# The head of a streaming-encoder layer: where the modulation sums, the rotary tables and the LayerNorm scales are made

## The chip, the cores and the metric

One core of one Trainium2 chip runs the whole layer: batch 1, 512 positions, model width 1024, all in float32. The metric is the device time of one execution in microseconds (us); lower is better. The kernel before takes 1024.28 us (median of three runs, 1021.66 to 1024.99).

## What is computed

The layer has a token mixer and a gated MLP with a convolution. Both are modulated by a condition c, and both end in a residual LayerNorm. The change touches only what comes ahead of the token mixer's large matmuls: the modulation by c, the LayerNorm of x, the tables for the rotary embedding, and the first 704 columns of the input projection.

```python
def _rope_tables(pos):
    freqs = ROPE_THETA ** (-jnp.arange(0, QK_ROPE, 2, dtype=jnp.float32) / QK_ROPE)
    ang = pos.astype(jnp.float32)[..., None] * freqs
    return jnp.cos(ang), jnp.sin(ang)

def _modulate(x, shift, scale):
    return _layer_norm(x) * (1.0 + scale[:, None, :]) + shift[:, None, :]

def reference(x, c, pos, ...):
    cos, sin = _rope_tables(pos)
    c_act = jax.nn.silu(c)
    mod = c_act @ w_ada[l] + b_ada[l]
    sh_t, sc_t, gt_t, sh_f, sc_f, gt_f = jnp.split(mod, 6, axis=-1)
    h = _modulate(x, sh_t, sc_t)
    y = _token_mixer(h, cos, sin, w_in[l], ...)
    ...
```

Positions start at a random number up to 8191, so the angles have to be brought into one period before the sine is taken.

## The kernel before

A matmul in the kernel's precision is three passes: each operand is split into a high part (rounded to the fast float32 format) and a low part (what the rounding lost), and high times low, low times high and high times high are added in one PSUM bank. ScalarE (ACT) writes the high part, and VectorE (DVE) or GpSimd (POOL) subtracts to get the low part.

The head works in eight pieces, j = 0 to 7, one for each block of 128 channels of the model width. `first_loads(j)` (L177) issues on SyncE's queue (SP) four 256 KB tiles of the modulation weights (`ada`), which hold shift and scale columns of this block for all 1024 rows of c, and two tiles of input-projection weights (`w0`: 448 columns of latents, 256 columns of a gate). Tiles come from one pool of 48 buffers, so a load may have to wait until an older tile has been read for the last time.

`first_modulation(j)` (L186) makes the sum over c's rows on DVE: the weights lie with 128 rows on the partitions, and for each of the eight groups of rows one instruction multiplies a 128x256 half tile by a column of silu(c) and adds it to one of two running sums (two plain multiplications, L199, and six multiply-adds, L201). A last addition (L205) joins the two sums in `acc[0]`. The sum over the 128 partitions is still open then.

`prepare(j)` (L309) splits the `w0` weights (L318 on ACT, L319 on POOL), closes the sum over the partitions with two one-column matmuls against a column of ones (`pm`, L325; each call shows as two instructions in the trace), adds the bias on ACT (`md`, L330), transposes the normalised x of this block with four matmuls (`pt`, L336), and writes the modulated, transposed block twice on ACT (high part L342, full value L343) and its low part on POOL (L344). The split of piece j+1 is ordered behind the last split of piece j with `issue_after`, which adds an order on one engine and no wait between engines.

`first_columns(j)` (L349) adds the block to four banks of latents (`lat`, eight matmuls on the high part L355 and L356, four on the low part L357), and `first_gates(j)` (L359) to two banks of a gate (`g0ps`, six matmuls, L97 to L99). All eight pieces add into the same banks, so these are complete only after piece 7. Then the kernel goes on with gate columns (`pg`), the latents' norms, rotary queries and attention.

Ahead of the pieces, x is loaded in eight tiles, DVE takes its statistics (L134, L122), and for each of the four row blocks POOL makes reciprocal root and offset in three tiny instructions (L113, L116, L125). ACT normalises the first half of x's columns (L219), POOL the second (`late_norm`, L229). Two `warm` matmuls (L225) follow the normalised tiles. The rotary tables (L379 to L413) are made on DVE behind the fifth modulation sum: 14 instructions reduce the angles (L393 to L398), two sines run on ACT (L404, L411), and two scaled copies on DVE (L412, L413).

The order of the instructions on each engine is a planner's: it runs its own model of time over the whole program and takes what is ready there by its place in the program, with the `issue_after` marks as fixed order. On the chip each engine then runs its list in that order, and an instruction that waits holds up all behind it.

Of the kernel before, what the change touches and what calls it, by code (L numbers as in the profile page):

```python
# [10 lines left out]
I32 = mybir.dt.int32  # L11
# [39 lines left out]
def trunk(ctx: ExitStack, tc: tile.TileContext, A, out):  # L51
# [95 lines left out]

# [7 lines left out]
    cols = const.tile([P, N_COLS], F32, name="cols")  # L155
    nc.scalar.dma_start(out=cols, in_=A["cols"])

# [13 lines left out]
    nc.vector.tensor_scalar_add(out=bmod[:, :, 1], in0=cols[:, C_SCT : C_SCT + 8], scalar1=1.0)  # L171

    first_raw = {}
    first_acc = {}
    add_done = []

# [9 lines left out]
    def first_modulation(j):  # L186
        adas, first_raw[j] = loads.pop(j)
        acct = act_t(f"acc{j}", F32)
        acc = [acct[:, :256], acct[:, 256:]]
        with ExitStack() as order:  # L190
            if add_done:
                order.enter_context(tc.issue_after(add_done[-1]))
            for q in range(4):
                ada = adas[q]
                for i in range(2):
                    k = 2 * q + i
                    src = ada[:, i * 256 : (i + 1) * 256]
                    if q == 0:
                        nc.vector.tensor_scalar_mul(out=acc[i], in0=src, scalar1=cact[:, k : k + 1])  # L199
                    else:  # L200
                        nc.vector.scalar_tensor_tensor(  # L201
                            out=acc[i], in0=src, scalar=cact[:, k : k + 1], in1=acc[i],
                            op0=ALU.mult, op1=ALU.add,
                        )
# [5 lines left out]
    kst = const.tile([P, N_CONST], F32, name="kst")  # L210
    nc.sync.dma_start(out=kst, in_=A["consts"])
    posi = const.tile([P, TT], I32, name="posi")
    nc.sync.dma_start(out=posi, in_=A["pos"])
    first_modulation(0)

# [1 line left out]
    xrs = [ln_stats(xs[t]) for t in range(TT)]  # L217
    for t in range(TT):
        nc.scalar.activation(  # L219
            xs[t][0], xs[t][0], AF.Identity, bias=xrs[t][:, 1:2], scale=xrs[t][:, 0:1]  # L220
        )

    warm = ps("warm")
    for t in (1, 2):
        nc.tensor.matmul(warm, ident, xs[t][0], start=True, stop=True)  # L225

    def late_norm():
        for t in range(TT):
# [6 lines left out]
    plan = []  # L235
# [32 lines left out]

# [1 line left out]
    def gate(b, m, pg=None):  # L270
# [28 lines left out]

# [1 line left out]
    lat = [ps(f"lat{t}") for t in range(TT)]  # L301
# [4 lines left out]
    split_done = []  # L306
    md_done = []

    def prepare(j):  # L309
        raws = first_raw[j]  # L310
        acc = first_acc[j]
        wh = wp.tile([P, D], F32R, name="w0h", tag="whi")
        wl = wp.tile([P, D], F32R, name="w0l", tag="wlo")
        with ExitStack() as order:
            for ins in split_done:
                order.enter_context(tc.issue_after(ins))
            for raw, a, b in ((raws[0], 0, NL), (raws[1], NL, NS)):
                nc.scalar.copy(out=wh[:, a:b], in_=raw[:, : b - a])  # L318
                nc.gpsimd.tensor_tensor(  # L319
                    out=wl[:, a:b], in0=raw[:, : b - a], in1=f(wh[:, a:b]), op=ALU.subtract  # L320
                )
        w0s.append((wh, wl))
        pm = ps("pm")
        for i in range(2):
            nc.tensor.matmul(  # L325
                pm[:, i : i + 1], acc[:, i * P : (i + 1) * P], ones[:, 0:1], start=True, stop=True
            )
# [5 lines left out]
        md_done.append(add_done[j])  # L333
# [12 lines left out]
        hT_hi.append(hh)  # L346
        hT_lo.append(hl)
# [29 lines left out]

# [1 line left out]
    with tc.issue_after(md_done[4]):  # L379
        posf = const.tile([P, TT], F32, name="posf")  # L380
        nc.vector.tensor_copy(out=posf, in_=posi)
        ang = const.tile([P, TT, 32], F32, name="ang")
        cosT = const.tile([P, TT, 32], F32, name="cosT")
        cosQ = const.tile([P, TT, 32], F32, name="cosQ")
        sinQ = const.tile([P, TT, 32], F32, name="sinQ")
        sinT = const.tile([P, TT, 32], F32, name="sinT")
        for t in range(TT):
            nc.vector.tensor_scalar_mul(
                out=ang[:, t, :], in0=kst[:, K_FREQ : K_FREQ + 32], scalar1=posf[:, t : t + 1]
            )  # L390
        kq = const.tile([P, TT, 32], F32, name="kq")
        for step in (COARSE, 1.0):
            nc.vector.tensor_scalar(  # L393
                out=kq, in0=ang, scalar1=INV_2PI, scalar2=MAGIC * step, op0=ALU.mult, op1=ALU.add
            )
            nc.vector.tensor_scalar_add(out=kq, in0=kq, scalar1=-MAGIC * step)
            for c2 in TWO_PI:
                nc.vector.scalar_tensor_tensor(  # L398
                    out=ang, in0=kq, scalar=-c2, in1=ang, op0=ALU.mult, op1=ALU.add
                )  # L400
        nc.vector.tensor_scalar(
            out=ang, in0=ang, scalar1=3.1415925, scalar2=-3.1415925, op0=ALU.min, op1=ALU.max
        )
        nc.scalar.activation(sinT, ang, AF.Sin)  # L404
        nc.vector.scalar_tensor_tensor(
            out=kq, in0=ang, scalar=-1.0, in1=ang, op0=ALU.mult, op1=ALU.max
        )
        nc.vector.tensor_scalar(
            out=kq, in0=kq, scalar1=-1.0, scalar2=1.5707963267948966, op0=ALU.mult, op1=ALU.add
        )  # L410
        nc.scalar.activation(cosT, kq, AF.Sin)  # L411
        nc.vector.tensor_scalar_mul(out=cosQ, in0=cosT, scalar1=SCALE)  # L412
        nc.vector.tensor_scalar_mul(out=sinQ, in0=sinT, scalar1=SCALE)  # L413


    th0 = [gate(0, m, g0psum[m]) for m in range(2)]
# [1 line left out]
    ss = const.tile([P, TT, 2], F32, name="ss")  # L418
# [55 lines left out]

# [1 line left out]
    qrs = []  # L476
# [51 lines left out]

# [1 line left out]
    V = {}  # L530
# [134 lines left out]

# [1 line left out]
    ada_state = {}  # L667
# [46 lines left out]

# [1 line left out]
    po_hi = [None] * KT  # L716
# [69 lines left out]

# [1 line left out]
    def uv_half(i, nm, hook=None):  # L788
# [56 lines left out]

# [1 line left out]
    sg_hi = []  # L847
# [79 lines left out]

# [1 line left out]
    lntg = row_tiles(2, act_t, "lntg")  # L929
# [211 lines left out]

# [1 line left out]
    pzs = {}  # L1143
# [203 lines left out]
```

## Time and profile before

| | |
|---|---|
| median of three runs | 1024.28 us |
| span of the profiled execution, first to last instruction | 1018.8 us |
| median less span (start and end outside the records) | 5.5 us |
| TensorE (PE) busy | 973.7 us, 96% of the span |
| VectorE (DVE) busy | 611.4 us, 60% |
| ScalarE (ACT) busy | 384.2 us, 38% |
| GpSimd (POOL) busy | 325.7 us, 32% |
| mean granted TensorE clock | 0.991 |

The profiled execution has no time of its own beside its span, so the span is set against the median of the runs. PE is busy nearly all the time, but its busy time is an upper figure, since matmuls overlap and their ends are modelled. What matters is the stretches in which it stands still, and these are listed by what ended them. DVE is the busiest engine of the first 62 us.

### The profile page before, as it was taken

The page shows a single profiled execution, that of the slowest core. Times are in us where ns is not written, and L with a number is a line of the kernel's source. Part 1 is how long each engine was busy: PE and PEld are TensorE (multiplying, and loading weights), DVE is VectorE, ACT ScalarE, POOL GpSimd, SP SyncE. Part 2 cuts the span into 40 slices and gives each one's busy share as a digit, 9 for nine tenths or more (in the row PEclk, how much of TensorE's full clock was granted, in tenths as well). Part 3 has the DMA queues.
Part 4 walks back from the last instruction along what each step waited for, and adds up shares of the span by engine and source line. Part 5 has one row for each costly group of instructions (what it writes and reads, how often), then busy time and mean ns, then how long its engine had stood idle before and what let it go on. Part 6 is the DMA issues. An engine that isn't in the chain of part 4 may idle for free.

```text
span 1018.8 us, 12189 instructions
## 1 busy us (share of the span) xinstructions
PE 973.7 (96%) x4496; PEld 797.4 (78%) x4496; DVE 611.4 (60%) x931; ACT 384.2 (38%) x650; POOL 325.7 (32%) x340
## 2 busy tenths in 40 slices
PE   4789999999999999999999999899999999999996
PEld 3677778777888877788888877898888888888885
DVE  7957555548446377763343578676666665633267
ACT  3365454542224322332322233664443443412221
POOL 5564111121242054120001575512111121466664
PEclk9999999999999999999999999999999999999998
DMA  9612111118324226652223255113433343342322
GB/s 336 259 40 91 47 50 50 57 42 279 114 83 124 89 80 211 202 184 87 79 83 104 83 169 203 42 62 113 136 124 112 116 145 85 99 137 94 103 83 83
DMA packets 45276, 119.20 MB, mean 117 GB/s; under 512 B 5280, under 2 KB 8736, under 8 KB 45216
## 3 DMA queue, kind: packets, MB, share of 16 engines
q1 hardware_dynamic: 45072, 118.30, 35.8%
q8 instruction: 35, 0.57, 0.2%
q14 instruction: 25, 0.20, 0.1%
q10 hardware_dynamic: 144, 0.12, 0.0%
HBM read 116.30 MB, written 2.10 MB: 116 GB/s over the span
## 4 chain that ended last, share of the span: by engine, by line
PE 73%; DVE 9%; POOL 6%; DMA 6%; issue 4%; ACT 2%; SPq 0%; DVEq 0%; POOLq 0%; ACTq 0%
PE pzu L97 7%; PE pzu L99 7%; PE pzu L98 7%; PE pg L98 4%; PE pyd L97 4%; PE pg L99 4%; PE pg L97 4%; PE pyd L99 4%; PE pyd L98 4%; PE pu L97 3%; PE pu L99 3%; PE pu L98 3%; PE py L98 2%; PE py L99 2%; PE py L97 2%
## 5 line engine op out<-in xcount | busy, mean ns | idle before, releaser
L1203 POOL TENSOR_TENSOR zc<-zc 128x512 f32<-128x512 f32 x22 | 32.8, 1489 | 178.9 <-ACT zc L1202 178.9
L936 POOL TENSOR_TENSOR d<-d,gtfb 128x512 f32<-128x512 f32 x44 | 72.8, 1677 | 41.9 <-DMA d<-in_wdn 39.5
L298 POOL TENSOR_TENSOR mg<-mg,th 128x512 f32<-128x512 f32 x16 | 25.0, 1562 | 139.7 <-DVE th L295 120.2
L1188 DVE SCALAR_TENSOR_TENSOR zc<-pzu,cols,zc 128x511 f32<-128x511 f32 x44 | 32.8, 747 | 52.4 <-ACT zc L1185 52.4
L1185 ACT ACTIVATE zc<-pzu,cols 128x512 f32<-128x512 f32 x44 | 34.2, 779 | 72.2 <-PE pzu L99 72.2
L941 DVE TENSOR_TENSOR dl<-d,dh 128x1024 fp32r<-128x1024 f32 x18 | 29.9, 1660 | 52.3 <-ACT dh L940 52.3
L679 DVE SCALAR_TENSOR_TENSOR ada<-adar,cact,ada 128x512 f32<-128x512 f32 x56 | 52.9, 970 | 13.2 <-DMA adar<-in_ada 13.2
L90 ACT CAST wbh<-wb 128x1024 fp32r<-128x1024 f32 x24 | 25.2, 1050 | 65.7 <-PE py L99 57.2
L91 DVE TENSOR_TENSOR wgl<-wg,wgh 128x1024 fp32r<-128x1024 f32 x22 | 27.3, 1243 | 35.3 <-ACT wgh L90 34.1
L91 DVE TENSOR_TENSOR wupl<-wup,wuph 128x1024 fp32r<-128x1024 f32 x38 | 46.6, 1227 | 0.0
L91 DVE TENSOR_TENSOR wbl<-wb,wbh 128x1024 fp32r<-128x1024 f32 x24 | 35.1, 1461 | 16.3 <-ACT wbh L90 16.1
L91 DVE TENSOR_TENSOR wsgl<-wsg,wsgh 128x1024 fp32r<-128x1024 f32 x16 | 19.6, 1223 | 39.4 <-ACT wsgh L90 39.4
L940 ACT CAST dh<-d 128x1024 fp32r<-128x1024 f32 x18 | 18.9, 1051 | 60.7 <-PE pyd L99 60.6
L90 ACT CAST wuph<-wup 128x1024 fp32r<-128x1024 f32 x38 | 39.5, 1039 | 0.0
L278 ACT ACTIVATE th<-pg 128x512 f32<-128x512 f32 x22 | 13.1, 597 | 61.8 <-PE pg L99 61.8
L113 POOL TENSOR_SCALAR pw<-mv 128x1 f32<-128x1 f32 x20 | 8.2, 408 | 82.5 <-DVE mv L122 69.6
L90 ACT CAST wsgh<-wsg 128x1024 fp32r<-128x1024 f32 x16 | 16.8, 1049 | 47.0 <-PE pu L99 44.9
L1192 DVE SCALAR_TENSOR_TENSOR zc<-pzu,cols,zc 128x510 f32<-128x510 f32 x44 | 32.7, 747 | 1.3
L936 POOL TENSOR_TENSOR o<-o,gttb 128x512 f32<-128x512 f32 x16 | 27.0, 1712 | 17.5 <-DVE th L295 9.8
L734 POOL TENSOR_TENSOR asum<-apad 128x527 f32<-128x527 f32 x8 | 9.1, 1141 | 59.2 <-ACT apad L729 25.9
L600 POOL TENSOR_SCALAR pe<-pe,mx 128x128 f32<-128x128 f32 (+3 forms) x32 | 17.4, 553 | 33.4 <-DVE mx L599 33.2
L201 DVE SCALAR_TENSOR_TENSOR acc<-ada,cact,acc 128x256 f32<-128x256 f32 x48 | 27.8, 638 | 0.0
(1369 smaller groups left out, 3230.0 us busy)
## 6 DMA issues: line engine op xcount, KB each, us to landing
wup<-in_wup SPq DMA_DIRECT2D x44, 512.0 KB, 3.5
adar<-in_ada SPq DMA_DIRECT2D x64, 256.0 KB, 3.8
wb<-in_wb SPq DMA_DIRECT2D x24, 512.0 KB, 3.5
wg<-in_wg SPq DMA_DIRECT2D x22, 512.0 KB, 3.5
d<-in_wdn SPq DMA_DIRECT2D x22, 512.0 KB, 3.5
ada<-in_ada SPq DMA_DIRECT2D x32, 256.0 KB, 4.8
wsg<-in_wsg SPq DMA_DIRECT2D x16, 512.0 KB, 3.5
wa<-in_wa SPq DMA_DIRECT2D x8, 512.0 KB, 3.5
```

The lines of the kernel that those rows point to most:

```text
L90: nc.scalar.copy(out=hi[:, :n], in_=raw[:, :n])
L91: nc.vector.tensor_tensor(out=lo[:, :n], in0=raw[:, :n], in1=f(hi[:, :n]), op=ALU.subtract)
L97: nc.tensor.matmul(o, wh, xl, start=start, stop=False)
L98: nc.tensor.matmul(o, wl, xh, start=False, stop=False)
L99: nc.tensor.matmul(o, wh, xh, start=False, stop=stop)
L679: nc.vector.scalar_tensor_tensor(out=acc[n], in0=src, scalar=cact[:, k : k + 1], in1=acc[n], op0=ALU.mult, op1=ALU.add,)
L936: nc.gpsimd.tensor_tensor(out=raw[:, c], in0=raw[:, c], in1=gt[n], op=ALU.mult)
L941: nc.vector.tensor_tensor(out=lo, in0=raw, in1=f(hi), op=ALU.subtract)
L1185: nc.scalar.activation(t, pz, AF.Identity, bias=cols[:, cc + 3 : cc + 4], scale=cols[:, cc + 2 : cc + 3])
L1188: nc.vector.scalar_tensor_tensor(out=t[:, 1:512], in0=pz[:, 0:511], scalar=cols[:, cc + 1 : cc + 2], in1=t[:, 1:512], op0=ALU.mult, op1=AL ...
L1192: nc.vector.scalar_tensor_tensor(out=t[:, 2:512], in0=pz[:, 0:510], scalar=cols[:, cc : cc + 1], in1=t[:, 2:512], op0=ALU.mult, op1=ALU.add,)
L1203: nc.gpsimd.tensor_tensor(out=val, in0=val, in1=gate, op=ALU.mult)
```

## The change

Six things change, all before the first gate columns:

1. The constants, the positions and the bias columns are loaded first, on ACT's queue. Before, constants and positions went on SP's queue behind the loads of piece 1.
2. The angles (position times frequency) are made on DVE ahead of x's statistics, their reduction right behind the statistics. The last three DVE steps and the two sines come in the loop's first turn, and the two scaled copies move from DVE to ACT.
3. For pieces 0 and 1 (`DIRECT = 2`) there is no DVE sum. `prepare` takes the raw weight tiles as stationary operands and a column of silu(c) as the moving one: eight matmul calls for shift and eight for scale, added in PSUM.
4. For pieces 2 to 7 the last addition (L205) goes. Both running sums are given to PE, which closes each of shift and scale with two calls in place of one.
5. The modulation of piece j+2 is entered in turn j, beside its loads, where before that of piece j+1 was.
6. LayerNorm's scales of x are made for two row blocks at a time: two POOL instructions and one DVE instruction where there were six on POOL. The second half of x is normalised on ACT, in the loop's second turn, where POOL did it before the loop.

```diff
+    kst = const.tile([P, N_CONST], F32, name="kst")
+    nc.scalar.dma_start(out=kst, in_=A["consts"])
+    posi = const.tile([P, TT], I32, name="posi")
+    nc.scalar.dma_start(out=posi, in_=A["pos"])
+    cols = const.tile([P, N_COLS], F32, name="cols")
+    nc.scalar.dma_start(out=cols, in_=A["cols"])
...
+    def sines():
+        nc.vector.tensor_scalar(
+            out=ang, in0=ang, scalar1=3.1415925, scalar2=-3.1415925, op0=ALU.min, op1=ALU.max
+        )
+        nc.scalar.activation(sinT, ang, AF.Sin)
...
+        nc.scalar.activation(cosT, kq, AF.Sin)
+        nc.scalar.activation(cosQ, cosT, AF.Copy, scale=SCALE)
+        nc.scalar.activation(sinQ, sinT, AF.Copy, scale=SCALE)
+
+    angles()
...
     def first_modulation(j):
         adas, first_raw[j] = loads.pop(j)
+        if j < DIRECT:
+            first_acc[j] = [
+                (adas[q][:, i * 256 : (i + 1) * 256], cact[:, 2 * q + i : 2 * q + i + 1])
+                for q in range(4) for i in range(2)
+            ]
+            return
...
-            add = nc.vector.tensor_tensor(out=acc[0], in0=acc[0], in1=acc[1], op=ALU.add)
-        add_done.append(add.ins)
-        first_acc[j] = acc[0]
+        last_acc[:] = [ins.ins]
+        first_acc[j] = [(a, ones[:, 0:1]) for a in acc]
...
+    def x_scales(a, b):
+        power(rsx[:, a:b, 0], mvx[:, a:b, 1], 1.0, LN_EPS, b - a)
+        nc.vector.scalar_tensor_tensor(
+            out=rsx[:, a:b, 1], in0=mvx[:, a:b, 0], scalar=-1.0, in1=rsx[:, a:b, 0],
+            op0=ALU.mult, op1=ALU.mult,
+        )
...
+    for t in range(TT):
+        stats = x_stats(t)
+        if t % 2:
+            x_scales(t - 1, t + 1)
+            for u in (t - 1, t):
+                x_norm(u, 0)
     first_modulation(0)
...
+    first_modulation(1)
+    with tc.issue_after(stats.ins):
+        for step in (COARSE, 1.0):
+            reduce_angles(step)
...
     def late_norm():
-        for t in range(TT):
-            nc.gpsimd.tensor_scalar(
-                out=xs[t][1], in0=xs[t][1], scalar1=xrs[t][:, 0:1], scalar2=xrs[t][:, 1:2],
-                op0=ALU.mult, op1=ALU.add,
-            )
+        with after_split():
+            for t in range(TT):
+                x_norm(t, 1)
...
         pm = ps("pm")
         for i in range(2):
-            nc.tensor.matmul(
-                pm[:, i : i + 1], acc[:, i * P : (i + 1) * P], ones[:, 0:1], start=True, stop=True
-            )
+            for part, (a, col) in enumerate(acc):
+                nc.tensor.matmul(
+                    pm[:, i : i + 1], a[:, i * P : (i + 1) * P], col,
+                    start=part == 0, stop=part == len(acc) - 1,
+                )
...
     prepare(0)
-    late_norm()
     for j in range(KT):
         if j + 2 < KT:
             loads[j + 2] = first_loads(j + 2)
-        if j + 1 < KT:
-            first_modulation(j + 1)
+            first_modulation(j + 2)
+        if j == 0:
+            with after_split():
+                sines()
+        if j == 1:
+            late_norm()
         first_columns(j)
```

## Rows read from the trace of the kernel before

**Rows 1.** Busy time of each engine by stretches of the whole span (stretch in us: its length, then busy us and instructions of each engine, granted TensorE clock, share of the DMA engines, GB/s).
```profile
0.00:69.50 69.50, 47.36 (x213) 38.64 (x214) 57.67 (x111) 29.59 (x70) 38.38 (x53) 0.98 0.61 219
69.50:200.00 130.50, 129.67 (x636) 103.01 (x635) 75.17 (x177) 68.72 (x161) 32.84 (x78) 1.00 0.19 62
```

**Rows 2.** The chain of waits that ended last, from 11 to 70 us, in order of time (start us, length us, what).
```profile
61.93 0.44 DVE acc L205
...
62.41 0.61 PE pm L325 x4
```

**Rows 3.** What PE waited for between 30 and 66 us (us in total, times, longest).
```profile
PE pm L325 <- DVE acc L205: 8.1, 4, 2.6
PE lat L355 <- ACT hT5h L342: 0.4, 1, 0.4
```

**Rows 4.** The timeline, PE's matmuls alone (start us, length us, line, operation; the step from one start to the next is what a matmul costs in a row).
```profile
19.43 0.71 PE L355 MATMUL lat<-w0l,hT0h 128*128 128x448 f32 x1 [1.02 <-POOL w0l L319]
...
22.55 0.85 PE L325 MATMUL pm<-ones,acc 128*128 128x1 f32 x4
23.26 0.92 PE L336 MATMUL pt<-ident,x 128*128 128x128 f32 x4
...
26.21 0.50 PE L325 MATMUL pm<-ones,acc 128*128 128x1 f32 x4
26.57 0.45 PE L355 MATMUL lat<-w0l,hT1h 128*128 128x448 f32 x1
...
28.65 1.06 PE L357 MATMUL lat<-w0h,hT1l 128*128 128x448 f32 x4
...
34.16 0.72 PE L355 MATMUL lat<-w0l,hT2h 128*128 128x448 f32 x1
...
37.76 1.06 PE L357 MATMUL lat<-w0h,hT2l 128*128 128x448 f32 x4
...
40.04 0.50 PE L325 MATMUL pm<-ones,acc 128*128 128x1 f32 x4
...
44.75 0.36 PE L355 MATMUL lat<-w0l,hT4h 128*128 128x448 f32 x1
...
65.53 0.36 PE L355 MATMUL lat<-w0l,hT7h 128*128 128x448 f32 x1
...
69.33 0.39 PE L97 MATMUL pg<-hT0l,wgh 128*128 128x512 f32 x1
```

**Rows 5.** Stretches of 1 us, columns as in rows 1; then PE's weight loads by line (operation, count, busy us, mean ns of one).
```profile
21.00:22.00 1.00, 1.00 (x4) 0.87 (x4) 1.00 (x2) 0.00 (x0) 1.00 (x2) 1.00 0.98 369
35.00:36.00 1.00, 1.00 (x4) 0.87 (x4) 1.00 (x3) 0.00 (x0) 0.00 (x0) 0.50 1.05 408
...
L356 PEld LDWEIGHTS lat<-w0h,hT0h 128*128 128x128 f32 x4 | 1.3, 331 | 0.1
...
L356 PEld LDWEIGHTS lat<-w0h,hT1h 128*128 128x128 f32 x4 | 0.8, 189 | 0.1
```

**Rows 6.** The one-column matmuls by the tile they write: duration ns min/median/max, first and last start.
```profile
L325 PEld LDWEIGHTS pm<-ones,acc x32: 185/192/334, 15.8 to 62.7; 128*128 128x128 f32 x32
L325 PE MATMUL pm<-ones,acc x32: 164/250/352, 16.6 to 62.8; 128*128 128x1 f32 x32
```

**Rows 7.** Groups of DVE, POOL and ACT instructions from 0 to 66 us (busy us, mean ns of one, idle before).
```profile
L201 DVE SCALAR_TENSOR_TENSOR acc<-ada,cact,acc 128x256 f32<-128x256 f32 x48 | 27.8, 638 | 0.0
L199 DVE TENSOR_SCALAR acc<-ada,cact 128x256 f32<-128x256 f32 x16 | 11.5, 757 | 0.0
L398 DVE SCALAR_TENSOR_TENSOR ang<-kq,ang 128x128 f32<-128x128 f32 x10 | 5.7, 573 | 0.2
...
L319 POOL TENSOR_TENSOR w0l<-w,w0h 128x448 fp32r<-128x448 f32 x8 | 10.2, 1273 | 0.2 <-ACT w0h L318 0.2
L319 POOL TENSOR_TENSOR w0l<-w,w0h 128x256 fp32r<-128x256 f32 x8 | 6.6, 824 | 0.0
L344 POOL TENSOR_TENSOR hT1l<-hfull,hT1h 128x512 fp32r<-128x512 f32 x1 | 1.3, 1287 | 2.6 <-ACT hfull L343 2.6
...
L318 ACT CAST w0h<-w 128x448 fp32r<-128x448 f32 x8 | 4.5, 563 | 3.6 <-issue 3.6
L330 ACT ACTIVATE md<-pm,bmod 128x1 f32<-128x1 f32 x16 | 3.3, 254 | 10.6 <-PE pm L325 10.6
L219 ACT ACTIVATE x<-x,rs 128x512 f32<-128x512 f32 x4 | 3.3, 813 | 8.8 <-POOL rs L125 7.5 <-DMA ada<-in_ada 1.3
L318 ACT CAST w0h<-w 128x256 fp32r<-128x256 f32 x8 | 3.2, 402 | 0.0
...
L404 ACT ACTIVATE sinT<-ang 128x128 f32<-128x128 f32 x1 | 0.3, 310 | 4.4 <-DVE ang L401 4.4
```

**Rows 8.** Two stretches: first the busy time of L201 alone (us, instructions), then of all engines (columns as in rows 1).
```profile
34.40:36.95 2.55, 2.45 (x6) 0.50 1.03 401
57.00:62.00 5.00, 4.83 (x6) 1.00 0.00 0
...
34.40:36.95 2.55, 2.55 (x8) 2.25 (x9) 2.52 (x8) 0.35 (x2) 0.00 (x0) 0.50 1.03 401
57.00:62.00 5.00, 3.20 (x16) 2.47 (x14) 4.97 (x8) 1.82 (x4) 3.59 (x3) 1.00 0.00 0
```

**Rows 9.** The timeline from 4 to 19 us, and the median time of the modulation loads from issue to landing (last row: count, KB, us).
```profile
4.66 2.68 SPq L180 DMA_DIRECT2D ada<-in_ada  x4
...
10.74 0.21 DVE L122 BATCH_NORM_AGGREGATE mv<-st 128x2 f32<-128x12 f32 x1
...
13.11 0.33 SPq L211 DMA_DIRECT2D kst<-in_consts  x1
...
13.80 0.79 POOL L116 TENSOR_TENSOR rs<-pw,neghalf 128x1 f32<-128x1 f32 x1
...
14.13 2.24 SPq L180 DMA_DIRECT2D ada<-in_ada  x4
...
14.74 2.07 PE L225 MATMUL warm<-x,ident 128*128 128x512 f32 x2 [1.19 <-ACT x L219]
...
15.77 0.81 ACT L219 ACTIVATE x<-x,rs 128x512 f32<-128x512 f32 x1 [1.08 <-POOL rs L125]
...
18.51 0.78 ACT L342 ACTIVATE hT0h<-pt,md 128x512 fp32r<-128x512 f32 x1 [0.60 <-PE pt L336]
...
ada<-in_ada SPq DMA_DIRECT2D x32, 256.0 KB, 4.8
```

More of the change, by code (lines that the diff above doesn't have):

```diff
@@ L154, in trunk @@
             )
-    cols = const.tile([P, N_COLS], F32, name="cols")
-    nc.scalar.dma_start(out=cols, in_=A["cols"])
     ident = const.tile([P, P], F32, name="ident")
@@ L171, in trunk, with angles, reduce_angles @@
     nc.vector.tensor_scalar_add(out=bmod[:, :, 1], in0=cols[:, C_SCT : C_SCT + 8], scalar1=1.0)
+    ang = const.tile([P, TT, 32], F32, name="ang")
+    kq = const.tile([P, TT, 32], F32, name="kq")
+    cosT, sinT, cosQ, sinQ = (
+        const.tile([P, TT, 32], F32, name=name) for name in ("cosT", "sinT", "cosQ", "sinQ")
+    )
+    def angles():
+        posf = const.tile([P, TT], F32, name="posf")
+        nc.vector.tensor_copy(out=posf, in_=posi)
+        for t in range(TT):
+            nc.vector.tensor_scalar_mul(
+                out=ang[:, t, :], in0=kst[:, K_FREQ : K_FREQ + 32], scalar1=posf[:, t : t + 1]
+            )
+    def reduce_angles(step):
+        nc.vector.tensor_scalar(
+            out=kq, in0=ang, scalar1=INV_2PI, scalar2=MAGIC * step, op0=ALU.mult, op1=ALU.add
+        )
+        nc.vector.tensor_scalar_add(out=kq, in0=kq, scalar1=-MAGIC * step)
+        for c2 in TWO_PI:
+            nc.vector.scalar_tensor_tensor(
+                out=ang, in0=kq, scalar=-c2, in1=ang, op0=ALU.mult, op1=ALU.add
+            )
+    def sines():
+        nc.vector.tensor_scalar(
+            out=ang, in0=ang, scalar1=3.1415925, scalar2=-3.1415925, op0=ALU.min, op1=ALU.max
+        )
+        nc.scalar.activation(sinT, ang, AF.Sin)
+        nc.vector.scalar_tensor_tensor(
+            out=kq, in0=ang, scalar=-1.0, in1=ang, op0=ALU.mult, op1=ALU.max
+        )
+        nc.vector.tensor_scalar(
+            out=kq, in0=kq, scalar1=-1.0, scalar2=1.5707963267948966, op0=ALU.mult, op1=ALU.add
+        )
+        nc.scalar.activation(cosT, kq, AF.Sin)
+        nc.scalar.activation(cosQ, cosT, AF.Copy, scale=SCALE)
+        nc.scalar.activation(sinQ, sinT, AF.Copy, scale=SCALE)
+    angles()
     first_raw = {}
     first_acc = {}
-    add_done = []
+    last_acc = []
+    DIRECT = 2
     def first_loads(j):
@@ L190, in first_modulation @@
         with ExitStack() as order:
-            if add_done:
-                order.enter_context(tc.issue_after(add_done[-1]))
+            for ins in last_acc:
+                order.enter_context(tc.issue_after(ins))
             for q in range(4):
@@ L200, in first_modulation @@
                     else:
-                        nc.vector.scalar_tensor_tensor(
+                        ins = nc.vector.scalar_tensor_tensor(
                             out=acc[i], in0=src, scalar=cact[:, k : k + 1], in1=acc[i],
@@ L225, in trunk, with after_split @@
         nc.tensor.matmul(warm, ident, xs[t][0], start=True, stop=True)
-    def late_norm():
-        for t in range(TT):
-            nc.gpsimd.tensor_scalar(
-                out=xs[t][1], in0=xs[t][1], scalar1=xrs[t][:, 0:1], scalar2=xrs[t][:, 1:2],
-                op0=ALU.mult, op1=ALU.add,
-            )
+    def after_split():
+        order = ExitStack()
+        for ins in split_done:
+            order.enter_context(tc.issue_after(ins))
+        return order
+    def late_norm():
+        with after_split():
+            for t in range(TT):
+                x_norm(t, 1)
     plan = []
@@ L306, in trunk @@
     split_done = []
-    md_done = []
     def prepare(j):
@@ L313, in prepare @@
         wl = wp.tile([P, D], F32R, name="w0l", tag="wlo")
-        with ExitStack() as order:
-            for ins in split_done:
-                order.enter_context(tc.issue_after(ins))
+        with after_split():
             for raw, a, b in ((raws[0], 0, NL), (raws[1], NL, NS)):
@@ L370, in trunk @@
             loads[j + 2] = first_loads(j + 2)
-        if j + 1 < KT:
-            first_modulation(j + 1)
+            first_modulation(j + 2)
+        if j == 0:
+            with after_split():
+                sines()
+        if j == 1:
+            late_norm()
         first_columns(j)
@@ L376, in trunk @@
         first_gates(j)
[L379 to L413, printed above, removed]
     th0 = [gate(0, m, g0psum[m]) for m in range(2)]
```

23 lines of the change are left out of this document (14 added, 9 removed).

## The prediction

> **What bounds the kernel now.** I read the busy times by stretches first [rows 1]. From 69.5 to 200 us PE is busy for 129.7 of 130.5, and nothing from there on is edited. In the first 69.5 us it is busy for 47.4, while DVE is busy for 57.7. The loss is in the head, and the edit is in the head.
>
> Next the chain of waits, to see which engine holds PE up [rows 2]. Toward the head's end it runs over DVE's sums (their last addition L205 at 61.93 for 0.44 us), and at 62.41 the one-column matmuls `pm` of the last piece start as that addition is done. PE's own waits say it outright [rows 3]: 8.1 us in four waits of `pm` for L205, and 0.4 us for a block that ACT wrote late. So the modulation sums on DVE set the pace of the eight pieces.
>
> Then PE's timeline, for what a piece costs when nothing is late [rows 4]. The cycle from 40.04 (`pm`) to 44.75 (first `lat` of the next piece) is clean: 4.71 us. Piece 0 takes 6.78 us (19.43 to 26.21), the rest of piece 7 takes 3.80 (65.53 to 69.33). Pieces 1 to 6 take 39.32 us (26.21 to 65.53), where six clean cycles would be 28.26. The excess is 11.1 us: 8.5 of waits; 1.5 because after one of them PE ran at the lower of its two levels (34.16 to 37.76 is 3.60 us for what took 2.08 from 26.57 to 28.65); the other 1.1 lies in restarts.
>
> The clock wants care. The granted clock reads 0.50 at 35 us, and 1.00 at 21 us, but weight loads of piece 0 (19.4 to 22.2 us) took 331 ns and those of piece 1 189 ns [rows 5]. I go by the loads, and by the steps of [rows 4], which are as long in piece 2: PE ran at 1.2 GHz from 19.4 to about 23.9 us and again from 33.7 to 37.7, each time after standing still, and otherwise at 2.4 GHz.
>
> **The change part by part.**
>
> *DVE's work falls (edits 2, 3, 4).* Pieces 0 and 1 leave DVE. Six pieces remain, each two L199 and six L201: 12 x 0.757 + 36 x 0.638 = 32.1 us [rows 7]. The first tile of piece 2 is issued at 14.13; without the two loads on SP from 13.11 on it is about 1 us earlier, and it lands 4.8 us after issue [rows 9]: 17.9. So DVE ends its sums near 50, where it ended at 62.4. The rotary steps must fit in front: ten L398 at 0.573 and some lighter ones, 6 to 8 us, between the last statistics (10.95) and 17.9. If they spill 1 us, the sums end at 51. PE's need comes later (below), so the waits go and with them the whole excess: **-11.1 us**. What is late next is PE itself.
>
> *Two more `pm` calls for pieces 2 to 7 (edit 4).* Four more instructions each, 0.09 us apiece at the full clock (26.21 to 26.57 for four) [rows 4]: 6 x 4 x 0.09 = **+2.2**. The dropped L205 is in the DVE sum above.
>
> *Raw weights for piece 1 (edit 3).* 16 calls, 32 instructions, 28 more than before: 28 x 0.09 = 2.5 us at full clock, 28 x 0.18 = 5.0 at the lower one (22.55 to 23.26 for four). Part can fill PE's pause ahead of the first `lat` (1.02 us idle before 19.43). Bounds 0 and 5.0; I take **+2.0**, near the full-clock price less some of the pause.
>
> *The start: raw weights for piece 0, batched scales, loads moved (edits 1, 3, 6).* x is ready earlier: the last statistics at 10.95, then POOL's two instructions (0.2 + 0.8), a small one on DVE (0.2) and two on ACT (2 x 0.81) give 13.8, against 16.58 before [rows 9]. But PE now has 32 `pm` instructions for piece 0, 5.8 us at the lower clock, and two warm calls of 2.07, from the first landing of the weights (4.66 + 4.8 = 9.5). In a row that ends at 19.4. Then 0.7 for the transposes (23.26 to 23.94) and 1.1 for ACT's block: first `lat` at 21.2. At best the 32 are done when x is, and `lat` starts at 15.6. Before it was 19.43, so -3.8 to +1.8; I take **+0.5**, toward the late end, since weights and x land together. The constants on ACT's queue stand ahead of `cols`, whose first reader is 3 us from being needed: nothing. DVE's angle steps run while it waits for x: nothing; if they didn't, 5 small steps, about 1.1 us, would delay the statistics.
>
> *The clock at the start.* PE has work from 9.5 on and no pause of more than about 1 us. The first piece cost 6.78 where 4.71 is clean, so between 0 and 2.1 us can come back. No row tells how PE's clock stands after a row of one-column matmuls; I take **-0.8**.
>
> *ACT takes over (edits 2, 6).* Per piece ACT has 0.56 + 0.40 + 2 x 0.25 + 2 x 0.78 = 3.0 us [rows 7, 9] of a PE cycle that is now 5.1. The four late norms add 4 x 0.813 = 3.25 in one turn, ahead of the next piece's split and block: 1.2 us beyond the free 2.1. Bounds 0 and 3.25; **+1.2**. The sines and copies, 4 x 0.31, fall in the pause of turn 0: nothing, unless DVE makes them behind a sum that waits for its load; ACT would then stand as it did before L404, 4.4 us [rows 7].
>
> *Turn order (edit 5)* changes only what the planner sees; nothing in itself.
>
> Sum: -11.1 + 2.2 + 2.0 + 0.5 - 0.8 + 1.2 = **-6.0 us**. The gates would then start at 63.3 instead of 69.33. PE is dense behind, and the latents' chain hangs on the same matmuls, so the shift should reach the end: span 1018.8 - 6.0 = 1012.8, plus the 5.5 us by which the median exceeds the span: **1018.3 us**. Check on DVE: before, the gates came 7.0 us after the last sum (62.37 to 69.33), now 7.3; PE wants the last sum by 56.0, and it is there by 50 or 51.
>
> **The rivals.**
>
> *A, DVE stays the bound.* Six L201 took 2.45 us with POOL silent and 4.83 while POOL was busy for 3.59: DVE loses 0.66 us per us of POOL [rows 8]. POOL keeps its splits, seven more pieces at 1.27 + 0.82 + 1.29 = 3.4 us, 23.7. If DVE lost all of POOL's time, its sums would be 6 x (6 x 0.41 + 2 x 0.33) = 18.7 plus 23.7 = 42.4 us, ending at 60.3; gates at 67.6, gain 1.7, time 1022.6. Against it: the loss in the row is two thirds, and the mean durations that I used contain it. For it: a denser PE draws POOL's work closer together. With a spill of rotary steps on top the gain goes to nothing. The Trainium skill's page "SBUF — State Buffer", section "Who interferes with whom", has this rule: a VectorE instruction with two SBUF inputs and a GpSimd instruction that reads SBUF exclude each other for the whole instruction. By it the full 23.7 would be lost and 1022.6 come out; the row agrees on the direction and shows two thirds of the size.
>
> *B, more comes back.* Piece 1's matmuls hide, the clock is up at the first `lat`, ACT has room: -11.1 + 2.2 - 2.1 - 2 = -13, cut by DVE's end (50 + 7.3 = 57.3, that is -12.0). Time 1012.3 to 1015. For it: PE's gap and the earlier x. Against: all must come together.
>
> *C, slower: the raw-weight matmuls become the start's bound.* Place: PE's list ahead of the first `lat`, if the planner puts piece 1's 32 instructions there too. Price: what each costs when its weights are not loaded under another. The rows give 0.18 between starts, 0.25 as median duration, 0.334 as the longest load [rows 6]. With 64 of them, warm 4.1, transposes 0.7 and block 1.1 from 9.5 on, `lat` starts at 15.4 + 64p. The rest saves 11.1 - 2.2 - 1.2 = 7.7, so it decides at 15.4 + 64p = 27.1, p = 0.183. At 0.25 the time is 1028.6, at 0.334 it is 1033.9. For it: such matmuls have only been seen in fours. Against: those fours went at 0.09 to 0.18.
>
> *D, the change works and the gain is eaten:* piece 1 exposed at the low clock (+3.0 on my sum) with the start at its late end: 1022 to 1024.
>
> **How the numbers follow.** My forecast, 3 to 9 us gained, has 0.53; B 0.15; A and D together 0.19, within 0.3% (3.1 us, about what a measurement here can tell); C 0.13. So faster 0.68, same 0.19, slower 0.13. The range runs from B's end, 1012.5, to 1026: it leaves out most of C and a little of B. The forecast's own is 1015 to 1021.
>
> **What would show it.** Right: PE's waits of `pm` for DVE nearly gone in the pieces, gates starting near 63, no group L205, `pm` at 112 instructions, DVE idle at some time before 60. Wrong: PE still waiting for `acc` (A); the first `lat` later than 24 us (C); ACT's late norms in the list ahead of a block for which PE waits more than 2 us; or a head that ends early and a later stretch that gives it back.

## The result and the profile after

Five runs of each kernel side by side: 1022.99 us before (1020.78 to 1024.99), 1027.52 us after (1026.0 to 1031.11). The ratio is 1.0049, 95% interval 1.0028 to 1.007: slower, where 1018.3 us was forecast and the range ended at 1026. The profiled execution of after took 1026.00 us, with a span of 1024.3 and a mean clock of 0.992, so 1.7 us lie outside the span. The 5.5 us that the table of before calls start and end outside the records are therefore mostly the distance of that one execution from the median.

Busy time by stretches of after, as in [rows 1]: first the head up to its gate columns and what follows, then two stretches of 10 us.

```profile
0.00:74.00 74.00, 60.96 (x293) 54.05 (x294) 38.26 (x87) 32.09 (x76) 30.53 (x41) 1.00 0.57 206
74.00:200.00 126.00, 125.17 (x612) 99.77 (x612) 72.00 (x170) 65.55 (x155) 32.83 (x78) 1.00 0.20 63
...
50.00:60.00 10.00, 10.00 (x59) 9.00 (x58) 0.00 (x0) 4.93 (x13) 5.95 (x7) 1.00 0.00 1
60.00:70.00 10.00, 10.00 (x58) 9.01 (x58) 0.00 (x0) 5.18 (x12) 5.93 (x7) 1.00 0.01 2
```

DVE fell from 57.7 to 38.3 us in the head and does nothing at all from 50 to 70 us. PE rose from 47.4 to 61.0 us in a head that is 4.5 us longer. What PE waited for in the first 80 us of after, and then what DVE waited for (us in total, times, longest):

```profile
PE warm L299 <- ACT x L281: 12.0, 1, 12.0
PE lat L431 <- ACT hT0h L418: 1.0, 1, 1.0
...
DVE wgl L91 <- ACT wgh L90: 23.3, 1, 23.3
```

Against [rows 3]: the 8.1 us of `pm` waiting for DVE are gone entirely. PE waits for x at the start, once for a block of ACT, and for nothing else. DVE stands idle for 23.3 us at the end of its sums. So the change does what it says, and still the head is longer. PE's timeline of after shows where (start us, length us, line, operation, count):

```profile
12.02 2.05 PE L299 MATMUL warm<-x,ident 128*128 128x512 f32 x2 [12.02 <-ACT x L281]
13.86 1.71 PE L401 MATMUL pm<-cact,ada 128*128 128x1 f32 x8
...
19.30 3.41 PE L401 MATMUL pm<-cact,ada 128*128 128x1 f32 x16
22.58 0.67 PE L412 MATMUL pt<-ident,x 128*128 128x128 f32 x2
24.27 0.71 PE L431 MATMUL lat<-w0l,hT0h 128*128 128x448 f32 x1 [1.02 <-ACT hT0h L418]
...
27.39 3.41 PE L401 MATMUL pm<-cact,ada 128*128 128x1 f32 x16
30.66 1.84 PE L433 MATMUL lat<-w0h,hT0l 128*128 128x448 f32 x4
32.30 3.41 PE L401 MATMUL pm<-cact,ada 128*128 128x1 f32 x16
...
36.31 0.78 PE L97 MATMUL g0ps<-hT0l,w0h 128*128 128x512 f32 x1
...
39.02 0.96 PE L401 MATMUL pm<-ones,acc 128*128 128x1 f32 x8
39.84 0.45 PE L431 MATMUL lat<-w0l,hT1h 128*128 128x448 f32 x1
...
44.98 0.45 PE L431 MATMUL lat<-w0l,hT2h 128*128 128x448 f32 x1
...
70.01 0.36 PE L431 MATMUL lat<-w0l,hT7h 128*128 128x448 f32 x1
...
73.82 0.39 PE L97 MATMUL pg<-hT0l,wgh 128*128 128x512 f32 x1
```

Three distances, each against [rows 4], account for the gates' shift of 73.82 - 69.33 = +4.5 us:

- the first `lat`: 24.27 against 19.43, **+4.8**;
- piece 0, first `lat` to the next piece's first `lat`: 15.57 against 7.14, **+8.4**;
- pieces 1 to 6: 30.17 (39.84 to 70.01) against 38.96 (26.57 to 65.53), **-8.8**. Piece 7 takes 3.81 as before.

The raw weights of piece 0 stand ahead of the first `lat`. Those of piece 1, 32 more instructions, stand inside piece 0, between its `lat` matmuls and behind them: 27.39 to 30.66 and 32.30 to 35.56. The weight loads of the tile `pm` of after, first those of the raw weights, then those of the closing matmuls (duration ns min/median/max, first and last start):

```profile
L401 PEld LDWEIGHTS pm<-cact,ada x64: 330/333/337, 13.0 to 35.3; 128*128 128x128 f32 x64
L401 PEld LDWEIGHTS pm<-ones,acc x48: 187/192/330, 38.6 to 65.5; 128*128 128x128 f32 x48
```

All 64 raw loads took 330 ns or more, as piece 0's did in [rows 5], and sixteen such matmuls take 3.27 us from one start to the next (27.39 to 30.66): 0.20 each. The closing matmuls later load in 192 ns. So from 12 to about 39 us PE ran at 1.2 GHz while it stood still for only 1 us. As in [rows 5], the granted clock's column reads 1.00 for all of this; the loads say otherwise. That is so in every profile here: the column reads 1.00 from the start until PE first comes up, whatever the loads are, and shows 0.50 only when PE falls again later (run 8 below has both side by side).

### The profile page after: what moved, and what is told of

Read it like the earlier page. It is cut to its first block, busy times and chain, and to the rows that moved or that the text cites. A ratio compares the mean times of both kernels' runs of the same rounds, so it can differ in the third digit from the quotient of the medians.

```text
span 1024.3 us, 12311 instructions
## 1 busy us (share of the span) xinstructions
PE 988.4 (96%) x4576; PEld 812.7 (79%) x4576; DVE 592.5 (58%) x907; ACT 386.7 (38%) x656; POOL 317.0 (31%) x328
## 4 chain that ended last, share of the span: by engine, by line
PE 75%; DVE 9%; DMA 5%; POOL 4%; issue 3%; ACT 2%; DVEq 0%; SPq 0%; POOLq 0%; ACTq 0%
PE pzu L97 7%; PE pzu L98 7%; PE pzu L99 7%; PE pyd L99 4%; PE pyd L98 4%; PE pyd L97 4%; PE pg L99 3%; PE pg L98 3%; PE pg L97 3%; PE pu L97 3%; PE pu L99 3%; PE pu L98 3%; DMA adar<-in_ada 3%; PE py L99 2%; PE py L97 2%
## 5 line engine op out<-in xcount | busy, mean ns | idle before, releaser
L90 ACT CAST wuph<-wup 128x1024 fp32r<-128x1024 f32 x38 | 39.5, 1039 | 0.0
L90 ACT CAST wgh<-wg 128x1024 fp32r<-128x1024 f32 x22 | 23.2, 1052 | 11.6 <-PE pu L99 5.7
```

The source lines that it names most:

```text
L90: nc.scalar.copy(out=hi[:, :n], in_=raw[:, :n])
```

## The experiments

The theory after this reading: PE's own list is the bound, the 64 raw instructions cost some 13 us at 1.2 GHz where before eight closing ones did that work, and DVE was relieved far beyond need. The rivals: the moved rotary steps or the dropped additions are to blame, or PE's clock alone. Ratios are of the runs to those of the kernel before on the same chip, with 95% intervals; "gates" is the start of the first `pg`, 69.33 before and 73.82 after.

**1 and 2. No raw piece; only piece 0 raw.** The change with `DIRECT` as a set of pieces.

```diff
-    DIRECT = 2
+    DIRECT = ()
...
-        if j < DIRECT:
+        if j in DIRECT:
```

> The changed kernel with no piece on raw weights: DVE makes all eight sums, all else stays. If the 64 one-column matmuls of pieces 0 and 1 cost the time, the first lat starts at 18 to 20 us (24.3 in the changed kernel), the second piece's first lat at 26 to 28 (39.8), PE waits for DVE's sums again, the gates start at 66 to 69 (74.0), and the time is 0.996 to 1.001 of before. Rival, the start is late because of the loads or the batched scales: first lat at 22 or later, gates at 71 or later, 1.002 or more.

> Only piece 0 on raw weights. If the cost is the one-column matmuls at 0.2 us apiece, half of it stays: first lat still near 24, but the second piece's first lat near 32 and the gates near 68, 0.998 to 1.000 of before. If only piece 1's place in the list does harm, the gates are at 66 or less; if only piece 0's, at 72 or more.

No raw piece: 1.0000 [0.998, 1.0021], gates 69.78. Piece 0 alone (`DIRECT = (0,)`): **0.9959 [0.9944, 0.9973]**, 1019.38 us, gates 66.86. PE's timeline with piece 0 alone:

```profile
24.45 0.71 PE L431 MATMUL lat<-w0l,hT0h 128*128 128x448 f32 x1 [1.02 <-ACT hT0h L418]
...
28.83 0.63 PE L412 MATMUL pt<-ident,x 128*128 128x128 f32 x4
...
32.30 0.45 PE L431 MATMUL lat<-w0l,hT1h 128*128 128x448 f32 x1
```

The first `lat` is where it is in after, so piece 1's raw weights don't delay it. Without any raw piece it comes at 20.22. But the second piece begins at 32.30 in place of 39.84: piece 1's raw weights cost 7.5 us inside piece 0. Thirty-two at 0.20 are 6.4, and they take the place of eight closing ones, some 1; the other 2 are the rest of the piece at the lower level. Here the four transposes at 28.83 already have the short length (0.63; at 35.56 in after four took 1.09); there PE came up only at about 39.0. One raw piece turns the loss into a gain of 0.4%. Without any, PE waits for late blocks and for DVE in the first pieces, as the waits of the kernel with no raw piece show:

```profile
PE lat L433 <- POOL hT1l L420: 2.3, 1, 2.3
PE pm L401 <- DVE acc L254: 1.8, 1, 1.8
```

**3. Raw weights alone on the kernel before**, for pieces 0 and 1. The closing matmuls loop over a list, as in the change; the rest is as it was, rotary steps and last additions among it.

```diff
+        if j < 2:
+            first_acc[j] = [
+                (adas[q][:, i * 256 : (i + 1) * 256], cact[:, 2 * q + i : 2 * q + i + 1])
+                for q in range(4) for i in range(2)
+            ]
+            return
```

> The kernel before with raw weights for pieces 0 and 1 and nothing else of the change. If they alone make the loss: one-column steps of 0.18 to 0.20, second piece's first lat at 37 to 41, PE with next to no wait for DVE behind it, gates at 71 to 75, 1.002 to 1.006 of before. Rival, they do harm only together with the other edits: gates at 68 or less, 0.999 or less.

0.9995 [0.998, 1.001]: no change, where 1.002 or more was expected if the raw pieces alone make the loss. First `lat` at 23.43, second piece at 38.59, gates at 70.32. The raw pieces alone make 4.0 us of the 4.8 by which the start is late in after; the other 0.8 stand ahead of them, where the first warm call waits for x until 12.02 in after and until 11.09 here. And alone they take away every wait for DVE in the pieces. Its pieces go at 4.72 us (43.27 to 47.99), against 5.17 in after. So with two raw pieces the dropped additions buy nothing.

**4. The additions back on DVE**, one pair of closing calls for pieces 2 to 7; the rest of the change stays.

```diff
+            ins = nc.vector.tensor_tensor(out=acc[0], in0=acc[0], in1=acc[1], op=ALU.add)
         last_acc[:] = [ins.ins]
-        first_acc[j] = [(a, ones[:, 0:1]) for a in acc]
+        first_acc[j] = [(acc[0], ones[:, 0:1])]
```

> The changed kernel with the last addition of pieces 2 to 7 back on DVE, so that PE closes each with two calls. DVE stood still from 48 us on in the changed kernel, PE never waited for it. Theory: the additions cost nothing there and their place on PE 0.46 us a piece: cycle 4.71 instead of 5.17, gates at 70.8 to 71.4 (73.8), 1.000 to 1.003 of before. Rival: DVE is still short and the gates stay at 73 or later, 1.004 or more.

1.0005 [0.9993, 1.0017]: it takes back nearly the whole loss. PE's timeline of this kernel:

```profile
43.97 0.50 PE L402 MATMUL pm<-ones,acc 128*128 128x1 f32 x4
44.34 0.45 PE L432 MATMUL lat<-w0l,hT2h 128*128 128x448 f32 x1
...
71.35 0.39 PE L97 MATMUL pg<-hT0l,wgh 128*128 128x512 f32 x1
```

Four closing instructions in 0.37 us, where after has eight in 0.80 (44.18 to 44.98); six pieces at 0.43 are 2.6 us, and the gates come 2.5 us earlier. PE still never waits for DVE's sums, and DVE is still idle for 18.8 us. With two raw pieces edit 4 is a cost and nothing else. By the ratios the time falls by more than the gates, 4.5 us; the two intervals leave some 2.5 us either way.

**5. The rotary steps behind DVE's last sum**, no raw piece.

```diff
-    angles()
...
+    with tc.issue_after(last_acc[-1]):
+        angles()
+        for step in (COARSE, 1.0):
+            reduce_angles(step)
+        with after_split():
+            sines()
```

> No raw piece, and the rotary tables moved behind DVE's last sum; the dropped additions, the batched scales and the moved loads stay. Theory: the rotary steps ahead of the sums ate what the dropped additions gave. Then the first lat is at 17 to 19.5, DVE ends its sums at 54 to 57, the gates start at 62 to 65, 0.991 to 0.996 of before. Rival, DVE's sums bind with or without them: gates at 68 or more, 0.999 or more.

**0.9953 [0.9937, 0.9968]**, 1017.21 us; against run 1, which differs in nothing else, the gates come at 63.01 in place of 69.78. In [rows 7] the rotary steps are DVE work ahead of the sums' end; in run 1 they stand between the first sums (from 11 to 25 us) and PE waits for it. With the sums first, the list of PE's waits has none for them. PE's timeline, then ACT's, show what comes next:

```profile
63.01 0.49 PE L97 MATMUL pg<-hT0l,wgh 128*128 128x512 f32 x1 [1.50 <-ACT wgh L90]
...
60.73 0.31 ACT L206 ACTIVATE sinT<-ang 128x128 f32<-128x128 f32 x1 [3.67 <-DVE ang L203]
...
61.93 1.03 ACT L90 CAST wgh<-wg 128x1024 fp32r<-128x1024 f32 x1
```

ACT stands for 3.67 us at the sine, and the gate's weights, queued behind it, come 1.5 us late. So edit 2 is the other half of the lost gain where DVE is the bound; with two raw pieces DVE has room, so it should not matter there, but no run tried that.

**6 and 7. Raw weights inside the dense stretch**, `DIRECT = (3, 4)` and `DIRECT = (3,)`.

> Two pieces on raw weights as in the change, but pieces 3 and 4, in the dense stretch. If the place at the lower clock made them dear, they run at 0.10 us a piece there, the gates start near 66, and the time is 0.995 to 0.999 of before. Rival, they cost 0.2 us wherever they stand, or pull the clock down: gates at 71 or later, 1.002 or more.

> Only piece 3 on raw weights, all else as in the change. One raw piece at 0.10 us a step costs PE 2.4 us and takes 5.3 off DVE: gates at 65.5 to 67.5 (68.3 with pieces 3 and 4, 69.8 with none), 0.996 to 0.999 of before. If raw pieces pay only at the front, where DVE waits for loads, gates stay at 68.5 or more.

Piece 3 alone: 0.9971 [0.9958, 0.9983], gates 66.92. Pieces 3 and 4: 1.0022 [1.0006, 1.0038], gates 68.27; here the gates come 1.1 us earlier than in before and the time is longer, against the expectation. Their loads take 192 ns throughout. Piece 3 alone, PE's timeline:

```profile
32.94 2.06 PE L401 MATMUL pm<-cact,ada 128*128 128x1 f32 x18
34.87 0.45 PE L431 MATMUL lat<-w0l,hT2h 128*128 128x448 f32 x1
```

Eighteen instructions in 1.93 us: 0.107 each, half of what they cost at the start, and PE is at 2.4 GHz before, in and after them. So the 32 instructions of a raw piece cost 3.4 us in a running PE. Their place, not their number alone, makes the price.

**8 and 9. PE brought up at the start**: nine dense matmuls into a bank that nothing reads, and then eleven.

```diff
+    hot = pt_t("hot")
+    nc.vector.memset(hot, 1.0)
+    heat = ps("heat")
+    for _ in range(9):
+        nc.tensor.matmul(heat, ident, hot, start=True, stop=True)
```

> The changed kernel with nine dense 512-column matmuls on constants ahead of everything on PE, to have the clock up when the raw weights come; their result is unused. If the one-column matmuls do not lower a clock that is up: steps of 0.10 us, first lat near 19, second piece's first lat near 28, gates near 62, time 0.993 to 0.996 of before. If the clock falls while they run: steps back to 0.20 after the first few, second piece's first lat at 35 or later, gates at 70 to 74, 1.002 to 1.005.

> Eleven dense matmuls at the start in place of nine, so that they reach the first warm call (12.8 us) and PE has no pause of 2.4 us ahead of it; else as the kernel with nine and nothing between. If the rows of one-column matmuls alone bring PE down: loads of 190 ns up to about 15.5 us, 330 ns from about 17 us on, raw steps of 0.20 us from then, first lat at 22.5 to 23.5, gates at 74 to 75.5. If the pause had brought it down: loads stay at 190 ns through piece 0's 32 raw instructions, these go at 0.10, first lat at 20 to 21, gates at 72 or earlier.

Nine: 1.0004 [0.9987, 1.0021], gates 74.53. They bring PE up, and then it falls again among the raw weights. PE's weight loads with nine, then a stretch (columns as in [rows 1]) in which the clock column shows the fall:

```profile
12.68 0.30 PEld L304 LDWEIGHTS warm<-x,ident 128*128 128x128 f32 x2 [2.40 <-ACT x L286]
...
14.59 1.05 PEld L406 LDWEIGHTS pm<-cact,ada 128*128 128x128 f32 x6
...
16.59 0.34 PEld L406 LDWEIGHTS pm<-cact,ada 128*128 128x128 f32 x1 [0.52 <-issue]
...
18.00:20.00 2.00, 2.00 (x11) 2.00 (x10) 1.62 (x5) 0.00 (x0) 0.00 (x0) 0.50 1.06 385
```

I read that first as the rows of one-column matmuls bringing the clock down. But there is a pause ahead of them: 2.40 us between two weight loads, 1.57 us in which PE does no matmul. With eleven it is filled, 1.0013 [0.9993, 1.0033], gates 71.67, and PE stays up through piece 0's raw rows. PE's timeline with eleven, then two stretches:

```profile
16.05 2.29 PE L406 MATMUL pm<-cact,ada 128*128 128x1 f32 x20
18.20 0.63 PE L417 MATMUL pt<-ident,x 128*128 128x128 f32 x4
19.86 0.71 PE L436 MATMUL lat<-w0l,hT0h 128*128 128x448 f32 x1 [1.02 <-ACT hT0h L423]
...
22.98 3.84 PE L406 MATMUL pm<-cact,ada 128*128 128x1 f32 x18
...
38.93 0.57 PE L437 MATMUL lat<-w0h,hT1h 128*128 128x448 f32 x1
...
18.50:19.00 0.50, 0.34 (x4) 0.10 (x1) 0.41 (x2) 0.36 (x3) 0.00 (x0) 1.00 1.03 381
19.00:20.00 1.00, 0.14 (x1) 0.17 (x2) 1.00 (x4) 1.00 (x2) 0.00 (x0) 0.52 1.09 390
```

Piece 0's raw rows go at 0.11 each (20 in 2.15 us), and the first `lat` comes at 19.86, 4.4 us earlier than in after. Then PE waits 1.02 us for the block, from 18.84 on, and is at the lower level. But the wait alone doesn't explain the fall: the column reads 1.00 up to 19.00 and 0.52 for the us after it, so the clock fell at about 19.04, 0.2 us into the wait and close behind the row of twenty that ended at 18.20. Through piece 1's raw rows, which cost 0.2 again, and all of piece 0 PE stays at the lower level until 39.5 us (the column reads 0.50 from 20 to 39), though it never stands still in between.

**10 and 11. Dense matmuls between the raw ones**: one of 512 columns behind every second raw call, with nine at the start (run 10) and without (run 11). They write the bank of the transposes, which these overwrite.

```diff
-                nc.tensor.matmul(
+                one = nc.tensor.matmul(
...
+                if j < DIRECT and part % 2:
+                    with tc.issue_after(one.ins):
+                        nc.tensor.matmul(pt, onesr, hot, start=True, stop=True)
```

> The changed kernel with the nine dense matmuls at the start, and one dense 512-column matmul (result unused) behind every second raw-weight call. If the long rows of one-column matmuls are what keeps PE at its lower level, the steps stay at 0.10 us in spite of 16 more matmuls, the second piece's first lat comes at 30 to 33 (39.1 with the nine alone), gates at 64 to 68, 0.994 to 0.998 of before. If the pause before 12.7 us lowered the clock, steps of 0.20, second lat at 40 or later, gates at 74 or later, 1.002 or more.

> The changed kernel with the dense matmuls between the raw-weight calls, without the nine at the start. If long rows of one-column matmuls keep the clock from rising, the mixed row raises it by itself: weight loads fall from 331 to 190 ns before piece 0's first lat, second piece's first lat at 33 to 36, gates at 67 to 70, 0.996 to 1.000 of before. If it needs the nine, the steps stay at 0.20 and the added 16 matmuls lengthen it: second lat at 41 or later, gates at 75 or later, 1.005 or more.

With both: **0.9954 [0.9936, 0.9972]**, 1018.02 us, gates 67.12: after's work with 25 more matmuls, and 6.7 us less at the gates. PE's weight loads:

```profile
23.52 0.33 PEld L442 LDWEIGHTS lat<-w0h,hT0h 128*128 128x128 f32 x1
23.89 0.86 PEld L409 LDWEIGHTS pm<-cact,ada 128*128 128x128 f32 x4
24.67 0.19 PEld L415 LDWEIGHTS pt<-hot,onesr 128*128 128x128 f32 x1
24.79 0.65 PEld L409 LDWEIGHTS pm<-cact,ada 128*128 128x128 f32 x4
```

Here too PE is at the lower level behind the wait of 1.02 us ahead of the first `lat` (21.14), but it is up again at 24.67, behind the first four of piece 1's raw instructions: from there on four load in 0.65, and the second piece begins at 33.23.

Between only: 1.006 [1.0038, 1.0082], 1027.86 us, gates 74.39. At the start PE stays at 1.2 GHz in spite of the dense ones. Four raw instructions and a dense one take 1.28 us there (14.02 to 15.31), where four in an unbroken row take 0.82; the first `lat` comes at 28.05. Its weight loads within piece 0:

```profile
30.43 0.33 PEld L439 LDWEIGHTS lat<-w0h,hT0h 128*128 128x128 f32 x1
30.80 1.13 PEld L406 LDWEIGHTS pm<-cact,ada 128*128 128x128 f32 x4
31.81 0.23 PEld L412 LDWEIGHTS pt<-hot,onesr 128*128 128x128 f32 x1
31.96 0.65 PEld L406 LDWEIGHTS pm<-cact,ada 128*128 128x128 f32 x4
```

Piece 0 begins as in after, at the lower level and after the same wait of 1.02 us; but PE is up at about 31.9 us, 3.9 us into the piece. In after it took until about 39.0, 14.7 us into it.

What this shows is how long PE stays down. In the five kernels in which unbroken raw rows stand in piece 0 while PE is at the lower level, it is down for 15 us from the first `lat` (after, runs 3 and 4) or 19 to 20 us (runs 8 and 9). Where these rows are not there or are broken by dense matmuls, it is 3 to 5 us (before, runs 2, 6, 7, 10 and 11), 9 us in run 1, and 7 us in run 5, counted from its fall at 19.2. So such rows, unbroken, keep PE down longer once it is; run 2 differs from after in piece 1's rows alone.

Two things stay open. The first dense matmul among piece 1's raw ones starts at 24.70 in run 10 and at 31.88 in run 11, as PE is coming up, so those in piece 0 did not bring it up; up to there piece 0 holds what it holds in after. And in runs 8 and 9 PE stays down for some 8 us more behind the last raw row, in dense matmuls and eight closing ones, where after needs 3.5 us. Nor is it shown that the rows cannot bring a running PE down: they ran at the higher level in runs 7 and 9, but both falls, in runs 8 and 9, came among or close behind them.

**12. A stacked version**: run 5 with the nine at the start and piece 4 raw.

> A try at a faster one: rotary tables behind the last sum, nine dense matmuls at the start for the clock, piece 4 alone on raw weights to end DVE's sums 5 us sooner. If the clock is up at the first lat, piece 0 takes 5 to 6 us instead of 8.35, one raw piece costs 2.4, no wait before the gates: gates at 60 to 62.5 (63.0 with rotary tables last alone), 0.992 to 0.995 of before. If the pauses ahead of the first lat drop the clock, or DVE can't follow: gates at 63 or later, 0.995 or more.

0.9985 [0.996, 1.0011], gates 63.80: a miss. PE's timeline has two waits of the same length for a block of ACT:

```profile
18.33 0.44 PE L430 MATMUL lat<-w0l,hT0h 128*128 128x448 f32 x1 [1.41 <-ACT hT0h L417]
...
30.02 0.64 PE L430 MATMUL lat<-w0l,hT2h 128*128 128x448 f32 x1 [1.41 <-ACT hT2h L417]
```

Behind the first PE is still at 2.4 GHz, and piece 0 takes 5.15 us where run 5 needs 8.35. Behind the second it is at 1.2 GHz: eight `lat` take 3.05 us in place of 1.69 behind the first. That, the second wait itself and piece 4's raw rows (3.3 us where eight closing instructions take 0.8) eat the gain, so the gates come no earlier than in run 5. A wait of this length does not by itself decide PE's level. Run 12's twelve executions spread from 1015.47 to 1027.32 us; the four longest have a mean clock of 0.986, the three shortest of 0.994.

**What the gates don't tell.** A profile shows one execution, and the stages behind the head add their own scatter: the medians of runs 6 and 12 lie some 3 us above what their gates promise, that of run 8, whose profiled execution is the longest of its ten, 5 us below. Where such a difference arises can be read from run 9's profiled execution (1027.21 us, mean clock 0.980, where its median is 1024.92). Its gates are 2.2 us ahead of after's, but its first `pzu` matmul comes at 648.7 against 646.8. The stretch from 600 to 650 us, after first and then run 9 (columns as in [rows 1]):

```profile
600.00:650.00 50.00, 45.55 (x204) 36.15 (x202) 39.99 (x54) 22.92 (x40) 31.53 (x34) 0.97 0.50 172
```

```profile
600.00:650.00 50.00, 44.13 (x190) 34.98 (x189) 38.40 (x54) 21.16 (x36) 29.84 (x34) 0.94 0.50 165
```

PE is busy for 1.4 us less there, at a lower clock: its waits for the mixer's residual rows (`pth` for `xr`) are 5.4 us against 3.0. What makes this wait longer in some executions wasn't tried, and stays open.

## Why the prediction was wrong, step by step

*What bounds the kernel before* was read rightly: DVE's sums, and the wait goes when DVE is relieved. *DVE's work falls* (-11.1) and *two more `pm` calls* (+2.2) were forecast at -8.9 together; pieces 1 to 6 gave -8.8. DVE's last sum was forecast for 50 or 51 and ended at 48.0. *ACT takes over* (+1.2) came to nothing: PE waits for no block in pieces 1 to 6.

**The step that failed is "Raw weights for piece 1 ... I take +2.0, near the full-clock price", with "The clock at the start ... I take -0.8"**: +1.2 together, where piece 0 measured +8.4. The prediction had itself read PE at 1.2 GHz in the place where these instructions would stand (19.4 to 23.9 us), so the lower-clock price was the one to take. The term's upper bound, 28 x 0.18 = 5.0, was also too low, for two reasons. A raw instruction in a row of sixteen costs 0.20 at 1.2 GHz, where fours had shown 0.18; that makes 32 x 0.20 - 4 x 0.18 = 5.7. And the rows delay PE's rise, so that the rest of piece 0 was paid at the lower level too (piece 0 took 6.78 for 4.71 before, [rows 4], and in after the six `g0ps` from 36.31 to 39.02 are 0.45 each, against 0.23 in the next piece). Run 2 prices the whole at 7.5 us; of it the raw instructions, less the closing ones that they replace, are 5.3, and the rest of the piece at the lower level some 2. "Part can fill PE's pause" was wrong outright: the pause of 1.02 us is still there at 24.27. And the clock's -0.8 counted on a PE that is up for part of piece 0. "Otherwise at 2.4 GHz" was misread: in before the four `pm` at 16.61 take 0.71 up to the next start, as those at 22.55 do, so PE had not been up ahead of 19.4 either.

The second failed term is *the start*, +0.5 with bounds of -3.8 to +1.8; it measured +4.8. Its own row of matmuls, laid end to end, said 21.2, and I chose 19.9. The row began at 12.02 and not at 9.5, since the first warm call stands ahead of the raw ones in PE's list and waits for x (2.5 us; the weights, too, were issued 0.9 later, at 5.57 in place of 4.66), and thirty-two at 0.20 are 0.6 more than at 0.18: 21.2 + 2.5 + 0.6 = 24.3. The error is to have taken the weights' landing as the start without asking what stands ahead of them in PE's list.

The sum by measured terms: -8.8 + 8.4 + 4.8 + 0 comes to +4.5 us before rounding, against -6.0.

**The rivals.** *C* was nearest: PE's list of raw weights as the bound. Its price fell at 0.20, above its break-even of 0.183; its place was off, since piece 1's instructions stand behind the first `lat` and not ahead. At 0.20 its own sum gives a loss of 1.1 us, where 4.5 was measured; it has no term for the rest of piece 0 at the lower level. With 0.13 it was priced as an outsider; for it spoke "such matmuls have only been seen in fours", which I counted as one doubt among others when it meant that no row priced the change's main addition. *A* never came up, as PE waited for no sum, but its row held: from 41.79 to 48.02 us six L254 took 6.23 us with POOL busy for 5.53, where six undisturbed took 2.45 [rows 8]; DVE lost 3.78, or 0.68 us per us of POOL, beside the row's 0.66. POOL lost some too: its two splits of `w0` take 2.20 us beside the sums (41.55, 45.13) and 1.85 once DVE is idle (50.23). The Trainium skill's page "SBUF — State Buffer", section "Who interferes with whom", has the two engines' instructions exclude each other. By that, as an estimate, all 5.53 us would be lost; here too the trace agrees on the direction and shows two thirds.

## What to carry to other kernels

Before work moves from an engine that is waited for to the engine that waits, count how much relief is needed: here one raw piece made the kernel 0.4% faster and the second made it 0.5% slower than before, while the relieved engine stood idle for 23 us. Put a row of one-column matmuls, each with weights of its own, where PE already runs at its higher level (0.107 us each here, 0.20 at the start), and take its price from rows of that length or measure it first. Read PE's level from the length of its weight loads, not from the clock column alone: ahead of PE's first rise the column read 1.00 while the loads took 330 ns.

## What the runs showed that I had not expected

- PE can be busy without a break and stay at 1.2 GHz: in after from 24.3 to about 39.0 us, with rows of sixteen one-column matmuls between eight, four and six dense ones. Without piece 1's rows it rose at 28.8 at the latest, 4.4 us into the piece (run 2).
- The same rows can run at the higher level throughout: 32 at 0.11 us in run 9, 18 in a row in run 7. What brings PE down is not settled: it is at the lower level behind a wait of 1.02 us in runs 9 and 10, and at the higher one behind the first wait of 1.41 us in run 12.
- Idle filler can pay: 25 matmuls without use made the changed kernel 9.5 us faster by the medians (1027.52 to 1018.02 us); 6.7 us of that show at the gates.
